# A two-layer recurrent trunk: the S5 branch loads a normed input that the GLA branch has written out

## The chip, the cores and the metric

The kernel runs on one core of one Trainium2 chip. The metric is the time of one execution on the device in microseconds (us). The kernel before takes 3261.68 us (median of three runs, 3260.92 to 3266.36).

The core has a matrix engine (TensorE, PE in the profile; PEld is its loading of weights), a vector engine (VectorE, DVE), a scalar engine (ScalarE, ACT), a general one (GpSimd, POOL), and SyncE (SP), which here issues nearly all DMAs. SBUF is the memory on the chip from which the engines work; DRAM is the large memory behind the DMAs.

## The reference, cut to what matters

One inference step of a trunk with two layers, on a prompt of 2048 tokens and 8 single sample tokens, with D_MODEL = 1024. The even layer norms its input, projects it, and runs two branches side by side on the same normed input: GLA (gated linear attention, 4 heads) and S5 (a diagonal state space model with 32 groups of 16 channels). Each branch ends in its half of one output projection, and both are added to the residual. The odd layer is a gated DeltaNet.

```
def rmsnorm(x, w):
    xf = x.astype(jnp.float32)
    y = xf * lax.rsqrt(jnp.mean(xf * xf, axis=-1, keepdims=True) + EPS)
    return (y * w.astype(jnp.float32)).astype(x.dtype)

h = rmsnorm(x, norm_w)              # both branches read this h
p = h @ w_in_even                   # q, k, v, r, gate code | S5 u, S5 gate
x = x + concat(gla(p) * silu(r), s5(p) * silu(gate)) @ w_out_even
```

The second half of this listing is written in short; the first is the reference's own text.

## The kernel before, in words

Tokens lie along the free axis as 2056 columns (8 samples, then 2048 of the prompt), features along the 128 partitions in 8 tiles of 128. Every product is made three times in parts to keep fp32 precision: a value is split into a high part (rounded to fp32r) and a low part (the rest), of the activations (`Hh`, `Hl`, or `Oh`, `Ol` for the output projection) and of the weights (`whl`), and PE adds hi*hi, hi*lo and lo*hi in one `pmm` tile (`dense_steps`, L93 in the profile). Weights are loaded as `raw` once, split by ACT (L319) and POOL (L320), stored to DRAM as `split` (L323), and loaded later from there as `whl` (L314, 512 KB each). `whl` has five buffers.

The even layer goes through the columns twice. GLA takes four blocks (520, 512, 512 and 512 columns): `gla_entry` transposes the input into `xT`, stores it in DRAM as `xs_d[0]` (L706), makes the norm's factor `rr`, stores one row of it in DRAM as `rr_d` (L716), makes the normed value `xn` (L721) and splits it into the block's tiles `Hh` and `Hl`. From there come GLA's products; `gla_out` ends the block: a product of `Oh`, `Ol` with the output weights, a load of the residual `res` (L1062, 256 KB), an addition on DVE (L1064), and a store to `xs_d[1]` (L1066). The addition reads the `pmm` tile, so it also frees it for PE.

S5 takes two halves. Half 0 has 1032 columns, worked in products of 392, 384 and 256 columns; half 1 has 1024, in two of 512. `s5_entry` makes the half's normed input again, in pieces of 264 or 256 columns: it loads `rr` (L1104) and, in two loads of 4 feature tiles, `xb` (L1107, 512 or 528 KB), and `normed` multiplies (POOL, L646), rounds to the high part (4 instructions on ACT, L648) and takes the low part (4 on DVE, L649). Then follow `s5_u` (the u products, the first with 392 columns), the scans, `s5_glu`, and the S5 half of the output projection (`ev` in `s5_glu`: load of `res` L1377, addition L1378, store to `xs_d[2]` L1379), whose tiles `oh`, `ol` are further buffers of the names Oh and Ol.

The order on PE is set by a weaver that runs these functions as generators side by side: a generator waits for an event that another posts, or says how many us its step is thought to take (the table `LAT`). The other engines are ordered by a scheduler from the same program. SP issues its DMAs in order on 8 lanes in turn; a DMA waits for the one eight before it, so at most eight are under way. The buffers `Hh`, `Hl` of S5 come free in half 0 when the last GLA chain closes its pool, and in half 1 when the glu products of half 0 (which keep `y5` and `yy` in the same two names) are done.

Of the kernel before, what the change touches and what calls it, by code (L numbers as in the profile page):

```python
# [35 lines left out]
C3 = float(np.float32(TWO_PI - C1 - C2))  # L36
MAGIC = 12582912.0

LAT = dict(gates=11, conv=5, kconv=8, snorm=5.25, z=2.04, tp=3, qtp=1, mt=18, grow=5, blocks=9, sub=3, dve=1.02, act=0.675,
           gchain=0.9, gload=1.2, gsample=15, columns=0.9, hout=3, gsplit=3.57, inv1=1.53, inv2=1.3, inv3=0.9,  # L40
           inv4=0.837, inv5=0.796, inv6=0.972, chain1=0.972, chain2=0.729, chain3=0.837, split=1.95, sload=2.66,
           cout=2.25, norm=5.5, load=2, us=3.74, sq=4, out=3.24, entry=9.6, x=1.88, gentry=7.98, make=30, far=8,
           pr=1.5, gate=9, lvl1=4.73, lvl=1.8, gnorm=6.8, scan=2.33, tab=10, entry5=8, glu=3, gelu=1.5, ysum=6)
LEAD = (750, 400)
HA, HL, GA = 6, 6, 2
SMB = 3
# [93 lines left out]
def tile_trunk(ctx, tc, A, O):  # L140
# [27 lines left out]
    def pieces(blk):  # L168

        ns, off, T, _ = bounds(blk)  # L170
        out, o = [], 0
        for c in range(0, blk[1], 2):
            k = min(2, blk[1] - c)
            w = P * k + (ns if c == 0 else 0)
            out.append((o, w, c, k))
            o += w
        return out
# [98 lines left out]


    xs_d = [dram.tile([P, KD, TT], F32, name="xs_d%d" % i) for i in range(3)]
    rr_d = dram.tile([1, TT], F32, name="rr_d")
    yp_d = dram.tile([S, D], F32, name="yp_d")  # L280
    ys_d = dram.tile([NSM, D], F32, name="ys_d")
    vs_d = [dram.tile([NSM, GDV], F32, name="vs_d%d" % h) for h in range(GH)]
# [390 lines left out]
    def gla_entry(gp, blk):  # L673

        ns, off, T, subs = bounds(blk)
        hi = gp.tile([P, KD, TG], F32R, tag="Hh", name="Hh")
        lo = gp.tile([P, KD, TG], F32R, tag="Hl", name="Hl")
        HG[blk] = hi, lo
        cl = cols(blk)
        if blk[0] == 0:  # L680
            with tc.high_priority(offset=tc.cur_priority):
                xload(blk, 0)
                row0 = gp.tile([P, P], F32, tag="rr", bufs=2, name="row0")[:KD]
                nc.sync.dma_start(row0, A["norm_w"][0].rearrange("(n p) -> n p", p=P))
                for j in range(1, len(cl)):
                    xload(blk, j)
                turn = vectors()
                pt = ptp()
                pe.transpose(pt[:, :KD], row0, ident[:KD, :KD])
                nc.vector.tensor_copy(nw0, pt[:, :KD])  # L690
        for j, (o, rows, ix) in enumerate(cl):
            x, xT = xload(blk, j), []
            if j:
                yield LAT["x"]
            for i4 in range(0, KD, 4):
                pt = ptp()
                p3 = pt[:, :4 * rows].rearrange("p (i t) -> p i t", i=4)
                for i in range(4):
                    pe.transpose(p3[:, i], x[:, (i4 + i) * P:(i4 + i + 1) * P], ident[:rows, :rows])
                tag = ("xT", "qe", "ket", "pt")[j % 4] if blk[0] == 0 else "xT"  # L700
                xT.append(gp.tile([P, 4, P], F32, tag=tag, bufs=2, name="xT")[:, :, :rows])
                if i4:
                    nc.vector.tensor_copy(xT[-1], p3)
                else:
                    nc.scalar.activation(xT[-1], p3, AF.Copy)
                nc.sync.dma_start(xs_d[0][:, i4:i4 + 4, off + o:off + o + rows], xT[-1])  # L706
            if j + 2 < len(cl):
                xload(blk, j + 2)
            yield LAT["pr"]
            if ix == 3:  # L710
                turn()
            pr = pmm()[:, :rows]
            pe.transpose(pr, rsx[:rows, ix:ix + 1].to_broadcast([rows, P]), ident[:rows, :rows])
            rr = gp.tile([P, P], F32, tag="rr", bufs=2, name="rr")[:, :rows]
            nc.scalar.activation(rr, pr, AF.Copy)
            nc.sync.dma_start(rr_d[0:1, off + o:off + o + rows], rr[0:1])  # L716
            for i4 in range(0, KD, 4):
                xn = gp.tile([P, 4, P], F32, tag="xn" if blk[0] else "kt", bufs=1 if blk[0] else 3,
                             name="xn")[:, :, :rows]
                for i in range(4):  # L720
                    nc.vector.scalar_tensor_tensor(xn[:, i], xT[i4 // 4][:, i], nw0[:, i4 + i:i4 + i + 1], rr,  # L721
                                                   op0=OP.mult, op1=OP.mult)
                split(hi[:, i4:i4 + 4, o:o + rows], lo[:, i4:i4 + 4, o:o + rows], xn,
                      nc.vector if blk[0] or i4 else nc.gpsimd)
            for (_, _, c, k) in subs:
                if blk[0] == 0 and c + k == ix:
                    weave.post(("gsub", c), LAT["gentry"])
                    weave.post(("gentry", 0))
        if blk[0] == 0:
            chunk_mask()  # L730
            pmask.update({s: block_mask(s, False, "pm%d" % s) for s in LEVELS})
        if blk[0]:
            weave.post(("gentry", GBLK.index(blk)), LAT["gentry"])
        yield LAT["gentry"]
        if blk[0]:
            yield "gz", GH * GBLK.index(blk) - 1
        yield from low_rank(gp, blk, hi, lo)
        weave.post(("lr", GBLK.index(blk)), LAT["dve"])
# [357 lines left out]
    def s5_entry(sp, half):  # L1096
        blk = SBLK[half]
        ns, off, T, subs = bounds(blk)
        hi = sp.tile([P, KD, TS], F32R, tag="Hh", name="Hh")
        lo = sp.tile([P, KD, TS], F32R, tag="Hl", name="Hl")  # L1100
        H5[half] = hi, lo
        for (o, w, c, k) in pieces(blk):
            rr = sp.tile([P, SWP], F32, tag="rr", bufs=1, name="rr")[:, :w]
            nc.sync.dma_start(rr, rr_d[0:1, off + o:off + o + w].to_broadcast([P, w]))  # L1104
            for i4 in range(0, KD, 4):
                xb = sp.tile([P, 4, SWP], F32, tag="xb", bufs=2, name="xb")[:, :, :w]
                nc.sync.dma_start(xb, xs_d[0][:, i4:i4 + 4, off + o:off + o + w])  # L1107
                normed(hi[:, i4:i4 + 4, o:o + w], lo[:, i4:i4 + 4, o:o + w], xb, rr, nw0[:, i4:i4 + 4], nc.vector)
            yield 0.0

    def s5_u(sp, half, ct, late):
# [214 lines left out]
    def s5_glu(sp, half):  # L1326
# [39 lines left out]
        yield from blocks_steps(A["s5_w_glu"][0], 4, 4, yh, yl, subs, ev_glu)  # L1366
        weave.post(("glu", half))
        if last:
            sp.close("sil", "entry", "main", "early")
            dp.open("main", "left")  # L1370
            weave.post("dnmain")
        sq = sp.tile([P, TS], F32, tag="sq", bufs=1, name="sq")
# [18 lines left out]
        if ns:  # L1391
# [7 lines left out]

    apart = dict(out=("xin", "thr", "res"), out2=("Oh", "Ol"), ext=("res2",))  # L1400
    gp = Phase(tc, "gla", h=("Hh", "Hl"), **apart)
    sp = Phase(tc, "s5", early=("Hh", "Hl", "h0"), entry=("xb", "rr"),
               start=("Q", "rt", "rows", "ldt", "ev", "dt", "drow", "prm", "x0", "x1", "h0s", "hr"),
               tabs=("q", "kp", "pp", "v0", "v1", "bx", "by", "cx", "cy", "xx", "xy", "y1", "y2", "dd", "smI", "smC", "smR"),
               up=("upad", "bsm"), sq=("sq",), sil=("sil", "hn", "hm", "hos"), **apart)
# [39 lines left out]
    def gla_entries():  # L1445
        for i, blk in enumerate(GBLK):
            if i:
                yield "gtail", i - 1
            yield from gla_entry(gp, blk)
            if i == 0:  # L1450
                yield "gsample", GH - 1
            if i + 1 < nb:
                xload(GBLK[i + 1], 0)
                xload(GBLK[i + 1], 1)
# [17 lines left out]
    def gla_chains():  # L1472
        for g, blk, h in gsteps:
            yield "gpre", g
            yield from gla_chain(gp, blk, h, g)
            weave.post(("gchain", g), LAT["gsplit"])
        for h_ in range(GH):
            nc.sync.dma_start(O[2][0, 0, h_], gS[h_])
        gp.close("main")
        sp.open("early", "left")  # L1480
        sp.open("entry", "left")
        weave.post("early5")

    def gla_outs():
# [24 lines left out]
    def s5_dense():  # L1509
        yield "early5"  # L1510
        yield "tabs"
        sp.open("sq", "right")
        sp.open("sil", "right")
        S5["h0"] = sp.tile([P, 2, SG, NSM], F32, tag="h0", bufs=1, name="h0")
        nc.sync.dma_start(S5["h0"], h0_d)
        delta_masks()
        for half in range(len(SBLK)):
            if half:
                yield "glu", half - 1
                yield "hn", half - 1  # L1520
                sp.close("up")
                sp.open("entry", "left")
            yield from s5_entry(sp, half)
            if half == 0:
                sp.close("entry")
                sp.open("main", "left")
                sp.open("up", "left")
            weave.post(("main5", half))
            yield LAT["entry5"]
            late = []  # L1530
            for ct in range(4):
                yield from s5_u(sp, half, ct, late)
            for ct in range(4):
                yield from after(s5_sg(sp, half, ct), late)
            weave.post(("H5", half))
# [805 lines left out]
```

## Time and profile before

| | before |
|---|---|
| median of three runs | 3261.68 us (3260.92 to 3266.36) |
| the profiled execution | 3250.56 us |
| its span, first to last instruction | 3248.8 us |
| PE busy | 2955.9 us, 91% of the span |
| DVE, ACT, POOL busy | 2224.4, 1255.7, 995.0 us |
| DMA | 602.96 MB, mean 186 GB/s |

The profile is one execution. Its busy times are sums per engine; the views by stretch and by wait say where PE stood and for whom. Times are from the span's start. The even layer takes about the first 1500 us: the GLA blocks start at about 0, 400, 650 and 900 us, S5's half 0 at 1174 us and half 1 at 1425 us.

### The profile page before, as it was taken

The page shows a single profiled execution, that of the slowest core. Times are in us where ns is not written, and L with a number is a line of the kernel's source. Part 1 is how long each engine was busy: PE and PEld are TensorE (multiplying, and loading weights), DVE is VectorE, ACT ScalarE, POOL GpSimd, SP SyncE. Part 2 cuts the span into 40 slices and gives each one's busy share as a digit, 9 for nine tenths or more (in the row PEclk, how much of TensorE's full clock was granted, in tenths as well). Part 3 has the DMA queues.
Part 4 walks back from the last instruction along what each step waited for, and adds up shares of the span by engine and source line. Part 5 has one row for each costly group of instructions (what it writes and reads, how often), then busy time and mean ns, then how long its engine had stood idle before and what let it go on. Part 6 is the DMA issues. An engine that isn't in the chain of part 4 may idle for free.

```text
span 3248.8 us, 53026 instructions
## 1 busy us (share of the span) xinstructions
PE 2955.9 (91%) x18425; PEld 2497.5 (77%) x18425; DVE 2224.4 (68%) x5715; ACT 1255.7 (39%) x3321; POOL 995.0 (31%) x1236
## 2 busy tenths in 40 slices
PE   6888799999999989978988888899998999999998
PEld 5877678777778768877767888877887788787886
DVE  7766556645444546765867888867887678857885
ACT  5443343323323323241134444443444344434442
POOL 6565444322202222240034444431112121211111
PEclk8898899999999999989999999999999999999999
DMA  7565965673483485664466566676444844475446
GB/s 216 190 209 177 297 184 148 190 256 126 136 276 126 133 287 153 200 202 148 155 198 216 172 193 185 190 230 221 139 147 140 270 146 145 125 234 192 141 139 191
DMA packets 398232, 602.96 MB, mean 186 GB/s; under 512 B 62521, under 2 KB 257964, under 8 KB 397828
## 3 DMA queue, kind: packets, MB, share of 16 engines
q1 hardware_dynamic: 394902, 589.98, 57.3%
q0 software_dynamic: 2560, 8.42, 0.9%
q8 instruction: 145, 2.38, 0.3%
q10 hardware_dynamic: 502, 1.17, 0.1%
q14 instruction: 123, 1.01, 0.1%
HBM read 433.31 MB, written 166.34 MB: 185 GB/s over the span
## 4 chain that ended last, share of the span: by engine, by line
PE 35%; DVE 15%; DMA 4%; issue 3%; ACT 2%; POOL 1%; SPq 0%; POOLq 0%; DVEq 0%; ACTq 0%
PE pmm L93 23%; PE prc L93 5%; PE ptp L97 2%; PE pch L93 2%; DVE yc L1692 2%; PE ppo L93 2%; DVE z L1237 1%; DVE z L1247 1%; DVE Hl L649 1%; DMA out<-yt 1%; DMA LB<-md_d 1%; DVE z L1243 1%; DMA whl<-split 1%; DVE z L1238 0%; DVE z L1248 0%
## 5 line engine op out<-in xcount | busy, mean ns | idle before, releaser
L93 PE MATMUL pmm<-Hh,whl 128*128 128x512 f32 (+4 forms) x5200 | 1597.3, 370 | 42.8 <-ACT pre L1682 13.2
L93 PEld LDWEIGHTS pmm<-Hh,whl 128*128 128x128 f32 x5200 | 951.2, 193 | 173.8 <-ACT pre L1682 14.8
L93 PE MATMUL pmm<-Hl,whl 128*128 128x512 f32 (+5 forms) x2640 | 937.0, 355 | 5.6 <-DVE Hl L649 4.2
L93 PEld LDWEIGHTS pmm<-Hl,whl 128*128 128x128 f32 (+1 forms) x2640 | 506.5, 192 | 55.6 <-DVE Hl L649 6.0
L93 PE MATMUL pmm<-Oh,whl 128*128 128x512 f32 (+2 forms) x1120 | 354.3, 379 | 30.5 <-DVE res L1064 13.4
L320 POOL TENSOR_TENSOR whl<-raw,whl 128x512 fp32r<-128x512 f32 (+1 forms) x176 | 232.3, 1322 | 203.9 <-ACT whl L319 194.9
L93 PEld LDWEIGHTS pmm<-Oh,whl 128*128 128x128 f32 x1120 | 211.3, 200 | 65.7 <-DVE res L1064 16.9
L1692 DVE SCALAR_TENSOR_TENSOR yc<-pre,cvec,yc 128x512 f32<-128x512 f32 (+1 forms) x288 | 228.8, 795 | 43.2 <-ACT yc L1690 40.5
L93 PE MATMUL pmm<-Ol,whl 128*128 128x512 f32 (+2 forms) x560 | 203.3, 363 | 0.6 <-DVE Ol L370 0.6
L319 ACT ACTIVATE whl<-raw 128x512 fp32r<-128x512 f32 (+1 forms) x176 | 108.5, 618 | 127.4 <-PE pmm L93 78.0
L93 PEld LDWEIGHTS pmm<-Ol,whl 128*128 128x128 f32 x560 | 112.6, 201 | 11.4 <-DVE Ol L370 1.7
L907 DVE TENSOR_TENSOR dlt<-b 128x512 f32<-128x512 f32 x112 | 87.5, 782 | 39.8 <-ACT E L914 38.9
L93 PE MATMUL pmm<-oh,whl 128*128 128x512 f32 (+3 forms) x320 | 93.6, 370 | 18.3 <-DVE res L1378 15.4
L908 ACT ACTIVATE E<-dlt 128x256 f32<-128x256 f32 x112 | 47.4, 423 | 156.1 <-DVE dlt L907 32.3
L1682 ACT ACTIVATE pre<-pmm 128x512 f32<-128x512 f32 (+1 forms) x120 | 61.1, 510 | 115.4 <-PE pmm L93 115.1
L646 POOL TENSOR_TENSOR xb<-xb,rr 128x1024 f32<-128x1024 f32 (+1 forms) x32 | 76.9, 2412 | 90.9 <-DMA xb<-xs_d 40.4
L1968 ACT ACTIVATE jk<-ppo,rq 128x128 bf16<-128x128 f32 x128 | 46.7, 365 | 140.2 <-PE ppo L93 139.1
L1685 POOL COPY halo<-pre 128x3 f32<-128x3 f32 x96 | 22.3, 232 | 241.0 <-ACT pre L1682 240.3
L1064 DVE TENSOR_TENSOR res<-pmm,res 128x512 f32<-128x512 f32 (+2 forms) x80 | 46.2, 584 | 68.6 <-PE pmm L93 50.0
L1729 ACT ACTIVATE jk<-ptp 128x128 bf16<-128x128 f32 x256 | 70.8, 277 | 53.8 <-PE ptp L97 48.3
L275 POOL TENSOR_TENSOR s<-s,mhalf 128x4 f32<-128x4 f32 (+2 forms) x41 | 40.6, 989 | 162.6 <-DVE s L274 160.7
L1695 ACT ACTIVATE th<-yc 128x512 f32<-128x512 f32 (+1 forms) x96 | 61.0, 635 | 73.1 <-DVE yc L1692 72.8
(1527 smaller groups left out, 6103.8 us busy)
## 6 DMA issues: line engine op xcount, KB each, us to landing
whl<-split SPq DMA_DIRECT2D x460, 512.0 KB
split<-whl SPq DMA_DIRECT2D x168, 512.0 KB
res<-xs_d SPq DMA_DIRECT2D x88, 256.0 KB
sm<-s5m SPq DMA_DIRECT2D x32, 514.0 KB
raw<-in_w_in_even SPq DMA_DIRECT2D x64, 256.0 KB
xs_d<-res SPq DMA_DIRECT2D x64, 256.0 KB
raw<-in_w_in_odd SPq DMA_DIRECT2D x64, 256.0 KB
LB<-md_d SPq DMA_DIRECT2D x64, 256.0 KB
```

Source lines behind the costliest of these rows:

```text
L93: return self.e.matmul(out, w, x, **kw)
L97: return self.e.transpose(out, x, ident)
L319: nc.scalar.activation(t[:, 0, :m], raw, AF.Copy)
L320: nc.gpsimd.tensor_tensor(t[:, 1, :m], raw, t[:, 0, :m].bitcast(F32), op=OP.subtract)
L646: nc.gpsimd.tensor_tensor(xb, xb, rr.unsqueeze(1).to_broadcast(list(xb.shape)), op=OP.mult)
L907: nc.vector.tensor_tensor(d3, b3, b3[:, :, s - 1:s].to_broadcast([P, nb_, 2 * s]), op=OP.subtract)
L908: nc.scalar.activation(E3[:, :, s:], d3[:, :, s:], AF.Exp, scale=IS)
L1682: nc.scalar.activation(pre[:, X0 + c * P:X0 + (c + k) * P], ps[:, n0:], AF.Copy)
L1692: nc.vector.scalar_tensor_tensor(yv, pre[:, i:W - 3 + i], convw[:, ti, i:i + 1], yv, op0=OP.mult, op1=OP.add)
L1695: nc.scalar.activation(t[:, 3:W], yv, AF.Tanh, scale=0.5)
L1729: nc.scalar.activation(jk, pt[:, c * P:(c + 1) * P], AF.Square, accum_out=ss[:, c:c + 1])
L1968: nc.scalar.activation(jk[:rows], po[:rows, c * P:(c + 1) * P], AF.Square, scale=rq[:rows, c:c + 1], accum_out=s1[:, c:c + 1])
```

## The change

`gla_entries` stores the block's tiles `Hh` and `Hl` to two new DRAM tensors `xn_d[0]` and `xn_d[1]`, in four steps of two stores each, a step thought to take `LAT["keep"]` = 15 us. That is 8 stores of 512 KB (520 KB in block 0) a block, 32 in all, 16.8 MB. `s5_entry` loads from there, per product's columns and per 4 feature tiles, the high and the low part: 12 loads in half 0 (four of 784 KB, four of 768 KB, four of 512 KB) and 8 of 1 MB in half 1, again 16.8 MB. Gone are, in S5, the 8 loads of `rr`, the 16 loads of `xb` (8.4 MB), 16 multiplications on POOL, 64 instructions on ACT and 64 on DVE, and in GLA the 17 stores of `rr_d`. The pool `entry` (buffers `xb`, `rr`) is gone, and with it the closing of that pool before `main` and `up` open. `normed` stays for the DeltaNet layer.

```
+            off, T = bounds(blk)[1:3]                        # gla_entries, after gla_entry(gp, blk)
+            for k in range(0, KD, 2):
+                yield LAT["keep"]
+                for t, to in zip(HG[blk], xn_d):
+                    nc.sync.dma_start(to[:, k:k + 2, off:off + T], t[:, k:k + 2, :T].bitcast(F32))
...
-            nc.sync.dma_start(rr_d[0:1, off + o:off + o + rows], rr[0:1])      # gla_entry
...
-        for (o, w, c, k) in pieces(blk):                                       # s5_entry
-            rr = sp.tile([P, SWP], F32, tag="rr", bufs=1, name="rr")[:, :w]
-            nc.sync.dma_start(rr, rr_d[0:1, off + o:off + o + w].to_broadcast([P, w]))
+        for (o, w, c, k) in subs:
             for i4 in range(0, KD, 4):
-                xb = sp.tile([P, 4, SWP], F32, tag="xb", bufs=2, name="xb")[:, :, :w]
-                nc.sync.dma_start(xb, xs_d[0][:, i4:i4 + 4, off + o:off + o + w])
-                normed(hi[:, i4:i4 + 4, o:o + w], lo[:, i4:i4 + 4, o:o + w], xb, rr, nw0[:, i4:i4 + 4], nc.vector)
+                for t, src in ((hi, xn_d[0]), (lo, xn_d[1])):
+                    nc.sync.dma_start(t[:, i4:i4 + 4, o:o + w].bitcast(F32), src[:, i4:i4 + 4, off + o:off + o + w])
             yield 0.0
...
-LAT = dict(... mt=18, grow=5, ... entry5=8, ...)
+LAT = dict(... mt=18, keep=15, grow=5, ... entry5=14, ...)
```

The order of PE's matmuls is the same before and after, instruction by instruction. SP's is not; three places follow. Line numbers of the changed kernel are lower by 1 (L1061, L1065) or by 4 (L1373, L1375).

SP, where S5's half 0 enters, before: `h` is the S5 state of the samples, `xb` and `rr` the inputs of the norm, `res` and `xs_d_86` the residual of the last GLA block.

```order
L1515 DMA h_11954<-h_d 128x512
L1104 DMA rr<-rr_d 128x264
L1107 DMA xb<-xs_d_85 128x4x264 x2
L1066 DMA xs_d_86<-res 128x512
L1062 DMA res<-xs_d_86 128x512
L314 DMA whl<-split_4804 128x1024
L314 DMA whl<-split_4921 128x1024
L1066 DMA xs_d_86<-res 128x512
L1062 DMA res<-xs_d_86 128x512
```

SP, the end of the same stretch in the changed kernel: 8 loads of the parts of the 384 and 256 columns, three of `sm<-s5m` and three of `sm<-s5k` (S5's tables), three of `whl`, four stores of `xs_d`, one `res` and `h` have gone ahead, 25 DMAs from the first `Hh` to the `split` shown, both included; `xn_d_88` is the high part, `xn_d_89` the low.

```order
L318 DMA raw<-in_w_in_even 128x4x128
L323 DMA split_12171<-whl 128x1024
L1104 DMA Hh<-xn_d_88 128x4x392
L1104 DMA Hl<-xn_d_89 128x4x392
L1104 DMA Hh<-xn_d_88 128x4x392
L1104 DMA Hl<-xn_d_89 128x4x392
L318 DMA raw<-in_w_in_even 128x4x128
L323 DMA split_12178<-whl 128x1024
L1065 DMA xs_d_86<-res 128x512
L1061 DMA res<-xs_d_86 128x512 x3
```

The first piece and the last residual loads of GLA stood near each other at the head; now the 392 columns, which PE's first u product reads, are the last of the twelve parts, and the last three residual loads stand behind them. The tables `sm` and the parts of the later columns stand ahead of both.

SP in GLA's block 2, before: `whl` are the output weights, `s5m` and `q` stores and loads of S5's tables.

```order
L318 DMA raw<-in_w_in_even 128x4x128
L1066 DMA xs_d_86<-res 128x512
L599 DMA s5m<-smR 128x258
L1066 DMA xs_d_86<-res 128x512
L314 DMA whl<-split_4686 128x1024
L1062 DMA res<-xs_d_86 128x512
L314 DMA whl<-split_4693 128x1024
L1062 DMA res<-xs_d_86 128x512
L528 DMA q<-s5q 128x68
```

The same place in the changed kernel.

```order
L318 DMA raw<-in_w_in_even 128x4x128
L599 DMA s5m<-smR 128x258
L1450 DMA xn_d_88<-Hh 128x2x512 x2
L1450 DMA xn_d_89<-Hl 128x2x512 x2
L314 DMA whl<-split_4689 128x1024
L1061 DMA res<-xs_d_86 128x512
L1065 DMA xs_d_86<-res 128x512
L314 DMA whl<-split_4696 128x1024
L528 DMA q<-s5q 128x68
L1450 DMA xn_d_88<-Hh 128x2x512 x2
L1065 DMA xs_d_86<-res 128x512
L614 DMA s5m<-smC 128x128
```

The block's eight stores stand between the loads of weights and residuals that the block's output products take, four, then four again. In block 1 they stand around two `whl` loads in the same way, in block 3 in one row with single DMAs between, and in block 0 all eight follow one another.

SP, where S5's half 1 enters, in the changed kernel: `xs_d_87<-res` are stores, `res<-xs_d_86` loads of half 0's S5 output products.

```order
L1104 DMA Hh<-xn_d_88 128x4x512
L1375 DMA xs_d_87<-res 128x384
L1104 DMA Hh<-xn_d_88 128x4x512 x2
L1104 DMA Hl<-xn_d_89 128x4x512
L1104 DMA Hh<-xn_d_88 128x4x512
L1375 DMA xs_d_87<-res 128x256
L1104 DMA Hl<-xn_d_89 128x4x512
L1375 DMA xs_d_87<-res 128x392
L1373 DMA res<-xs_d_86 128x256
```

The same place before.

```order
L1379 DMA xs_d_87<-res 128x384
L1107 DMA xb<-xs_d_85 128x4x256
L1377 DMA res<-xs_d_86 128x256
L1107 DMA xb<-xs_d_85 128x4x256
L1379 DMA xs_d_87<-res 128x256
L1377 DMA res<-xs_d_86 128x392
```

Six loads of 1 MB stand together ahead of the next residual load, where residual loads and loads of 512 KB took turns. Two more loads of `Hl` stand further up, the first of them ahead of the last load of `sil` (the gate of half 0's last glu product), and it waits until that product has read `yy`.

## Rows read from the trace of the kernel before

**Rows 1.** The page: busy times, then the first DMA queue.
```profile
PE 2955.9 (91%) x18425; PEld 2497.5 (77%) x18425; DVE 2224.4 (68%) x5715; ACT 1255.7 (39%) x3321; POOL 995.0 (31%) x1236
...
q1 hardware_dynamic: 394902, 589.98, 57.3%
```

**Rows 2.** Waits of PE, 1140 to 1260 us: us in total, times, longest.
```profile
PE pmm L93 <- ACT Hh L648: 9.3, 3, 6.3
PE pmm L93 <- DVE res L1064: 5.0, 3, 3.0
PE pmm L93 <- DVE Hl L649: 3.7, 3, 2.3
```

**Rows 3.** Timeline of PE: start, us, instructions, in brackets the idle time before.
```profile
1200.44 0.42 PE L93 MATMUL pmm<-Hh,whl 128*128 128x392 f32 x1 [1.27 <-DVE res L1064]
...
1213.14 0.69 PE L93 MATMUL pmm<-Hh,whl 128*128 128x384 f32 x1 [6.25 <-ACT Hh L648]
...
1214.14 0.84 PE L93 MATMUL pmm<-Hh,whl 128*128 128x384 f32 x2
...
1215.11 0.84 PE L93 MATMUL pmm<-Hh,whl 128*128 128x384 f32 x2
...
1218.44 0.51 PE L93 MATMUL pmm<-Hh,whl 128*128 128x384 f32 x2
...
1218.97 0.51 PE L93 MATMUL pmm<-Hh,whl 128*128 128x384 f32 x2
...
1231.16 0.34 PE L93 MATMUL pmm<-Hl,whl 128*128 128x392 f32 x1
```

**Rows 4.** Stretches of 10 us: PE, PEld, DVE, ACT, POOL, clock, DMA share, GB/s.
```profile
1200.00:1210.00 10.00, 5.06 (x24) 4.11 (x24) 5.79 (x8) 3.36 (x7) 5.16 (x3) 1.00 1.07 376
...
1220.00:1230.00 10.00, 4.77 (x22) 4.25 (x22) 5.43 (x8) 4.71 (x12) 5.22 (x3) 0.70 0.33 93
```

**Rows 5.** The norm's instructions by line: ns of one (min/median/max), first and last start.
```profile
L646 POOL TENSOR_TENSOR xb<-xb,rr x32: 2339/2392/2659, 1182.4 to 2835.9; 128x1024 f32<-128x1024 f32 x28, 128x1056 f32<-128x1056 f32 x4
...
L648 ACT ACTIVATE Hh<-xb,nw x64: 492/494/514, 1184.9 to 1469.2; 128x256 fp32r<-128x256 f32 x56, 128x264 fp32r<-128x264 f32 x8
...
L649 DVE SCALAR_TENSOR_TENSOR Hl<-xb,nw,Hh x64: 468/474/2665, 1185.5 to 1470.3; 128x256 fp32r<-128x256 f32 x56, 128x264 fp32r<-128x264 f32 x8
```

**Rows 6.** Timeline of SP at the start of half 0.
```profile
1174.18 2.67 SPq L1107 DMA_DIRECT2D xb<-xs_d  x2
```

**Rows 7.** Waits of DVE, 1165 to 1240 us.
```profile
DVE hn L1311 <- DMA h<-h_d: 6.0, 1, 6.0
```

**Rows 8.** Waits of PE, 1400 to 1520 us.
```profile
PE pmm L93 <- DVE res L1378: 11.0, 5, 5.2
PE ptp L97 <- DVE hos L1321: 6.1, 1, 6.1
PE pmm L93 <- ACT thr L1359: 3.8, 2, 2.1
```

**Rows 9.** The output products of half 0's S5 part, columns as in rows 4.
```profile
1430.00:1480.00 50.00, 39.00 (x221) 37.51 (x220) 34.28 (x61) 19.88 (x46) 18.99 (x10) 0.90 0.83 264
```

**Rows 10.** Stretches of GLA blocks 0, 1, 2, 3, columns as in rows 4.
```profile
40.00:60.00 20.00, 17.02 (x140) 16.09 (x138) 11.66 (x61) 15.02 (x26) 12.18 (x10) 1.00 0.54 170
400.00:440.00 40.00, 33.88 (x153) 26.14 (x154) 19.93 (x54) 15.39 (x33) 16.23 (x32) 0.87 0.78 242
630.00:700.00 70.00, 61.38 (x256) 45.24 (x257) 36.24 (x101) 18.95 (x47) 15.77 (x38) 0.93 0.89 287
900.00:970.00 70.00, 66.07 (x292) 50.62 (x291) 33.41 (x71) 19.79 (x39) 6.48 (x7) 1.00 0.87 287
```

**Rows 11.** Waits of PE, 0 to 1170 us.
```profile
PE pmm L93 <- DVE res L1064: 13.3, 7, 3.7
...
PE pmm L93 <- DMA whl<-split: 1.9, 2, 1.1
```

More of the change, by code (lines that the diff above doesn't have):

```diff
@@ L37 @@
 MAGIC = 12582912.0
-LAT = dict(gates=11, conv=5, kconv=8, snorm=5.25, z=2.04, tp=3, qtp=1, mt=18, grow=5, blocks=9, sub=3, dve=1.02, act=0.675,
+LAT = dict(gates=11, conv=5, kconv=8, snorm=5.25, z=2.04, tp=3, qtp=1, mt=18, keep=15, grow=5, blocks=9, sub=3, dve=1.02, act=0.675,
            gchain=0.9, gload=1.2, gsample=15, columns=0.9, hout=3, gsplit=3.57, inv1=1.53, inv2=1.3, inv3=0.9,
@@ L42 @@
            cout=2.25, norm=5.5, load=2, us=3.74, sq=4, out=3.24, entry=9.6, x=1.88, gentry=7.98, make=30, far=8,
-           pr=1.5, gate=9, lvl1=4.73, lvl=1.8, gnorm=6.8, scan=2.33, tab=10, entry5=8, glu=3, gelu=1.5, ysum=6)
+           pr=1.5, gate=9, lvl1=4.73, lvl=1.8, gnorm=6.8, scan=2.33, tab=10, entry5=14, glu=3, gelu=1.5, ysum=6)
 LEAD = (750, 400)
@@ L278, in tile_trunk @@
     xs_d = [dram.tile([P, KD, TT], F32, name="xs_d%d" % i) for i in range(3)]
-    rr_d = dram.tile([1, TT], F32, name="rr_d")
+    xn_d = [dram.tile([P, KD, TT], F32, name="xn_d%d" % i) for i in range(2)]
     yp_d = dram.tile([S, D], F32, name="yp_d")
@@ L1368, in s5_glu @@
         if last:
-            sp.close("sil", "entry", "main", "early")
+            sp.close("sil", "main", "early")
             dp.open("main", "left")
@@ L1401, in tile_trunk @@
     gp = Phase(tc, "gla", h=("Hh", "Hl"), **apart)
-    sp = Phase(tc, "s5", early=("Hh", "Hl", "h0"), entry=("xb", "rr"),
+    sp = Phase(tc, "s5", early=("Hh", "Hl", "h0"),
                start=("Q", "rt", "rows", "ldt", "ev", "dt", "drow", "prm", "x0", "x1", "h0s", "hr"),
@@ L1480, in gla_chains @@
         sp.open("early", "left")
-        sp.open("entry", "left")
         weave.post("early5")
@@ L1521, in s5_dense @@
                 sp.close("up")
-                sp.open("entry", "left")
             yield from s5_entry(sp, half)
             if half == 0:
-                sp.close("entry")
                 sp.open("main", "left")
```

## The prediction

> **What bounds the kernel now.** I read the page first: PE is busy for 91% of the span, DVE for 68%, the large DMA queue takes 57% of the DMA engines' time [rows 1]. So what the change takes from POOL, ACT and DVE counts only where PE stood waiting for it, and what it adds to the DMAs counts only where PE comes to wait for a transfer. Then I read PE's waits where the norm works. In half 0 PE waits 9.3 us for the high part (L648) and 3.7 us for the low part (L649), and 5.0 us for the additions of GLA's last residuals [rows 2]. PE's timeline shows what is lost: the first u product begins at 1200.44 us, its 384-column part comes 6.25 us late at 1213.14, and the second product begins just before 1231.16 [rows 3]. The stretches say that the DMAs are not idle meanwhile: in 1200 to 1210 their share is 1.07 at 376 GB/s; only in 1220 to 1230 is it down to 0.33 [rows 4]. I take 376 GB/s as the full rate. Last I read PE's waits around half 1 and the stretches in which the GLA blocks will make their stores; the reader is to look there for waits that the loads of residuals explain, and for room at the DMAs.
>
> **What goes.** 16 multiplications of 2.39 us on POOL (38 us), 64 instructions of 0.494 us on ACT (32 us) and 64 of 0.474 us on DVE (30 us) [rows 5]. None is itself on PE's path; the worth is PE's waits. The 17 small stores of `rr_d` are one SP issue each; I cost them at nothing.
>
> **Half 0.** How long would the first u product take if nothing held it? Three matmuls of 384 columns take 0.53 us at the full clock, from 1218.44 to 1218.97, so 0.46 ns a column, and 0.97 us at the half clock, 1214.14 to 1215.11, so 0.84 ns [rows 3]. The product is 24 matmuls over 1032 columns: 24 x 1032 x 0.46 ns = 11.4 us. It takes some 30.6 us now, so 19 us are lost, 13 in waits for the norm [rows 2] and the rest to the half clock after them.
>
> The change does not simply give these back. The loads start when the buffers come free, as the first `xb` does at 1174.18 [rows 6]. The order shows what stands ahead of the 392-column parts, which the first product needs first: 8.45 MB of parts in all, 2.0 MB of `sm` tables, 1.6 MB of `whl`, 1.0 MB of stores and 1.3 MB of other DMAs, 14.4 MB up to the last 392-column load; the first of the three last residual loads stands at 15.7 MB, two DMAs of weights and a store after them. At 376 GB/s these are 38 and 42 us, so the 392-column parts land at about 1212 and the residual at about 1216, some 1 to 2 later with what is under way when they start. The three additions that wait for those residuals each hold a `pmm` buffer, and the last GLA output product cannot start before one is free. So PE stops after the last but one output product (before, all were done at 1199) and resumes at about 1217.5. The last product's 12 matmuls of 512 columns take 12 x 512 x 0.84 ns = 5.2 us at the half clock, on which PE stands after such an idle time (1214.14 against 1218.44 [rows 3]), and then come 11.4 us of u, of which some us at the half clock add 1 to 2. The u product ends at 1235 to 1236 instead of 1231: **+4 us**. Bounds: at 10% more bytes per us everything comes 4 us earlier (0); with 3 us more of backlog and the state load of 6.0 us [rows 7] later for DVE too, +10. Below: if the residual loads are not what holds the last product, it runs beside the loads and u starts at 1212 to 1214, which ends it at 1224 to 1226, -6.
>
> The Trainium skill ("DMA: Bandwidth & Descriptors", Where 436 GB/s comes from) gives about 358 GB/s per core as what binds transfers between DRAM and SBUF, below the 435 of the fabric. The trace of this core shows 376 for 10 us [rows 4], so here the trace decides; by 358 the sum for half 0 would be 2 us worse.
>
> **Half 1.** The loads cannot start before half 0's glu products are read, as the order has it, at about 1418. The first `Hl` load now stands ahead of the last `sil` load and waits for that product; PE waited 3.8 us for `thr` here already [rows 8]; the sil load comes after 1 MB, 2.8 us at the full rate: I take +2. Then six loads of 1 MB stand ahead of the next residual load of the output products: 6.3 MB, 17 us; some four products' residuals are already in. With a product's share of the 50 us shown at some 2.8 us each I estimate that PE stands 7 us once. Against this the 11.0 us in which PE waited for the additions L1378 [rows 8], with L649 on the same engine between them, largely go, and POOL and ACT are free of 8 and 32 instructions. 2 + 7 - 11 = **-2 us**. Bounds: -11 (both costs hidden, all additions prompt) to +9 (both costs, nothing gained, because the additions were late for their loads: the share of the DMAs was 0.83 [rows 9]). The 6.1 us for `hos` [rows 8] are a chain between PE and DVE; I leave them.
>
> **GLA.** This is the part that the change's purpose does not speak of, and where I expect the loss. Each block gets 8 stores of 4.19 MB together (4.26 in block 0), 11.2 us of the full rate. They are read by nothing for long, but SP issues them in order between loads that PE's products wait for. I work out what room is there: 20 us at a share of 0.54 leave 9.2 us free in block 0, 40 us at 0.78 leave 8.8 in block 1, 70 us at 0.89 leave 7.7 in block 2, 70 us at 0.87 leave 9.1 in block 3 [rows 10]. In block 0 the stretch behind is as free and the weights run ahead: nothing. In the others 2.4, 3.5 and 2.1 us don't fit, and since five `whl` buffers are about as much prefetch as one burst of four stores delays (5 x 12 matmuls x 0.23 us = 14 us against 5.6), I charge just what doesn't fit: **+8 us**. Here whatever waits is a wait for `whl` (1.9 us so far) or for additions whose `res` comes late (13.3 us so far) [rows 11]. Bounds: 0, if the prefetch hides it all; +22, if blocks 2 and 3, whose output products take their weights and residuals at a share near 0.9, lose the whole 11.2 us each. Small gains from the missing `rr_d` stores I put at nothing.
>
> **Sum.** +4 - 2 + 8 = +10 us. The profiled execution took 3250.56 us and would take 3261; it is 11 us quicker than the median of the runs, to which I add the same 10: 3271.7, and I say **3271 us**.
>
> **The rivals.**
> 1. *The waits go and the stores are hidden (faster).* For it: PE waits 13 us for the norm in half 0 and 11 us for additions behind L649 in half 1 [rows 2, 8], and in the GLA blocks PE waited for `whl` only 1.9 us in 1170 us [rows 11], so prefetch has been deep enough. Against it: share 1.07 at 376 GB/s while the norm works [rows 4], and the residual loads behind the 392-column parts. Half 0 -4, half 1 -8, GLA +1: -11, 3251 us.
> 2. *No change.* The stores cost half of what I charge, half 0 comes out at 0, half 1 at -4: 0, 3262 us.
> 3. *The DMAs become the bound in GLA (much slower).* Blocks 2 and 3 lose the full 22 us, block 1 half of its 11.2, half 0 +4, half 1 -2: +30, 3292 us. It decides once the output products' loads stand at the full rate without the stores already; the shares of 0.87 to 0.89 are means over 70 us, with room in some places and none in others.
> 4. *The change does not remove the wait in half 0*, because it never was the norm's: the loads of `xb` are 4.2 MB, the parts are 8.45 MB, and they pass the same queue. This is inside my forecast and not a time of its own.
>
> The same skill page (Issuing engines are not separate DMA queues) says that all DMAs end on the same 16 engines, whoever issues them. That is a rule against moving work from three engines with room to the one resource that half 0 fills; no run here shows yet what it costs.
>
> **How the numbers follow.** My forecast 0.42, rival 1 0.30, rival 2 0.18, rival 3 0.10. A measurement of this kernel can tell about 0.2%, 6.5 us, from no change. The forecast's own range is 3262 to 3281, with one part in seven of it within 0.2%; a tenth of rival 1 lies there too. Faster 0.29, same 0.24, slower 0.47. The range that should hold 8 in 10 reaches from most of rival 1 to most of rival 3: 3247 to 3289 us.
>
> **What would show it.** In the profile after: the first u product should start near 1222 plus what the GLA blocks lost before it, with a wait of PE for the additions of GLA's residuals of 10 to 18 us in place of those for L648 and L649; if it starts before 1214 by that reckoning, the order of the loads does not matter. The waits of PE up to the start of half 0 should have grown by some 8 us, for `whl` or for `res` additions in blocks 2 and 3; if PE's work there ends at the same time as before, GLA costs nothing and rival 1 is near. In half 1 PE should have one wait of about 7 us for an addition whose `res` is late, and few others. I am wrong altogether if the GLA blocks change by more than 22 us, or if half 0 ends its u product more than 6 us earlier.

## The result, and the profile after

The changed kernel takes 3296.94 us (median of 6 runs, 3287.37 to 3306.56) where the kernel before takes 3259.86 in the same comparison: a ratio of 1.0124, 95% interval 1.0103 to 1.0146. It is slower, as forecast, but by some 37 us instead of 10, and above the range of 3247 to 3289 us. Its profiled execution took 3298.70 us, with a span of 3297.0.

PE runs its matmuls in the same order in both kernels, so the k-th matmul of one trace can be laid beside the k-th of the other, and the difference of their starts says how much later the changed kernel is at that place. This table is worked out that way from the traces: what each stretch of the first profile of before (its times head the columns) takes longer, in us. The second row is a second profile of before, and shows what is chance.

| | GLA, 0-1170 | half 0, 1170-1250 | 1250-1400 | half 1, 1400-1520 | 1520-1680 | DeltaNet, 1680-3240 | all |
|---|---|---|---|---|---|---|---|
| before, second profile (e5) | 3.7 | 0.2 | 1.8 | -2.2 | -0.8 | 12.5 | 15.2 |
| changed kernel | 19.6 | 8.3 | -1.1 | 13.9 | 0.2 | 7.4 | 48.4 |
| changed, second profile (e6) | 19.9 | 7.9 | -0.9 | 13.8 | -0.8 | 5.5 | 45.4 |

So the change costs about 8 us in half 0, 14 in half 1, and in GLA 16 to 20 of which a part is chance: e11 and e12 below have GLA's code as before and stand at 2.5 and -4.1 there. The DeltaNet layer, whose code is the same, takes 12 us longer in the second profile of before too: the first was a quick execution, and nothing there is the change's.

The page of the changed kernel, its busy times and first DMA queue: the three engines have less to do, as planned, by 34, 27 and 47 us [rows 1], and PE's work is the same within 6.

```profile
PE 2961.5 (90%) x18425; PEld 2501.3 (76%) x18425; DVE 2190.7 (66%) x5651; ACT 1228.8 (37%) x3257; POOL 948.2 (29%) x1220
...
q1 hardware_dynamic: 404532, 614.18, 58.3%
```

PE's waits in half 0 of the changed kernel, 1160 to 1260 us. Those for the norm [rows 2] are gone; in their place stand one of 17.8 us for an addition and 8.1 us for weights.

```profile
PE pmm L93 <- DVE res L1063: 20.7, 2, 17.8
PE pmm L93 <- DMA whl<-split: 8.1, 2, 5.7
```

DVE's waits, 1190 to 1250 us: the addition was late because its residual was, and the state load came 13.6 us late where it had been 6.0 [rows 7].

```profile
DVE res L1063 <- DMA res<-xs_d: 23.3, 2, 22.8
DVE hn L1307 <- DMA h<-h_d: 13.6, 1, 13.6
```

The stretches of half 0 and half 1 of the changed kernel, columns as in [rows 4]. Both show PE all but standing still while the DMAs run at a share above 1 and 349 to 398 GB/s; before, PE was still busy 4.77 us in its worst stretch [rows 4].

```profile
1200.00:1210.00 10.00, 4.26 (x17) 3.14 (x16) 0.69 (x1) 0.63 (x1) 1.28 (x1) 0.85 1.08 368
1210.00:1220.00 10.00, 7.11 (x23) 5.14 (x21) 1.88 (x4) 0.63 (x1) 1.27 (x1) 0.81 1.08 349
1220.00:1230.00 10.00, 1.86 (x7) 1.05 (x6) 0.00 (x0) 0.63 (x1) 0.92 (x1) 0.70 1.06 387
1230.00:1240.00 10.00, 0.00 (x0) 0.00 (x0) 0.00 (x0) 0.00 (x0) 0.34 (x1) 0.50 1.06 383
...
1460.00:1470.00 10.00, 1.41 (x8) 1.08 (x7) 0.00 (x0) 0.07 (x1) 2.67 (x3) 0.82 1.05 398
1470.00:1480.00 10.00, 2.47 (x8) 2.47 (x9) 0.84 (x2) 0.39 (x1) 0.00 (x0) 0.50 1.06 391
```

DVE's timeline in half 1: after the addition at 1457.90 the next has to wait until 1477.06 for its residual.

```profile
1457.90 0.56 DVE L1374 TENSOR_TENSOR res<-pmm,res 128x384 f32<-128x384 f32 x1 [0.39 <-PE pmm L93]
1459.02 0.55 DVE L1379 TENSOR_TENSOR sq<-sq,prc 128x384 f32<-128x384 f32 x1 [0.56 <-ACT prc L1377]
1477.06 0.42 DVE L1374 TENSOR_TENSOR res<-pmm,res 128x256 f32<-128x256 f32 x1 [17.48 <-DMA res<-xs_d]
```

PE's waits, 1420 to 1545 us: the additions' 11.0 us [rows 8] became 20.7; the waits for `hos` and `thr` grew by 1.3 and 0.3.

```profile
PE pmm L93 <- DVE res L1374: 20.7, 5, 16.1
PE ptp L97 <- DVE hos L1317: 7.4, 1, 7.4
PE pmm L93 <- ACT thr L1355: 4.1, 2, 3.3
```

The GLA blocks of the changed kernel, the stretches of [rows 10]: the shares of 0.54, 0.78, 0.89 and 0.87 are now 0.92, 0.96, 0.89 and 0.91, and PE is busy for 1.7 to 5.2 us less in each. The windows are those of the clock. Moved by the 9, 13.5 and 18.5 us by which PE is late there, the last three show shares of 0.96, 0.96 and 0.98, and PE is busy for 2.5, 4.7 and 1.2 us less.

```profile
40.00:60.00 20.00, 15.32 (x109) 14.51 (x108) 10.71 (x50) 14.96 (x23) 10.61 (x9) 0.83 0.92 333
400.00:440.00 40.00, 28.67 (x137) 22.47 (x136) 19.62 (x51) 15.28 (x32) 10.13 (x20) 0.86 0.96 320
630.00:700.00 70.00, 57.25 (x240) 42.02 (x241) 39.64 (x114) 18.65 (x52) 15.07 (x35) 0.90 0.89 293
900.00:970.00 70.00, 61.73 (x276) 47.00 (x276) 33.96 (x79) 14.71 (x36) 3.09 (x5) 0.98 0.91 309
```

### The profile page after: what moved, and what is told of

Same layout as the page of the kernel before. It is cut to its first block, busy times and chain, and to the rows that moved or that the text cites. A ratio compares the mean times of both kernels' runs of the same rounds, so it can differ in the third digit from the quotient of the medians.

```text
span 3297.0 us, 52863 instructions
## 1 busy us (share of the span) xinstructions
PE 2961.5 (90%) x18425; PEld 2501.3 (76%) x18425; DVE 2190.7 (66%) x5651; ACT 1228.8 (37%) x3257; POOL 948.2 (29%) x1220
## 4 chain that ended last, share of the span: by engine, by line
PE 35%; DVE 15%; DMA 5%; issue 3%; ACT 2%; POOL 1%; SPq 1%; POOLq 0%; DVEq 0%; ACTq 0%
PE pmm L93 24%; PE prc L93 5%; PE ptp L97 2%; PE pch L93 2%; PE ppo L93 2%; DVE yc L1690 2%; DMA out<-yt 1%; DVE z L1233 1%; DVE z L1243 1%; DMA LB<-md_d 1%; DMA xs_d<-res 1%; DVE z L1239 1%; DVE Hl L649 1%; DVE z L1234 0%; DVE z L1244 0%
## 5 line engine op out<-in xcount | busy, mean ns | idle before, releaser
L93 PEld LDWEIGHTS pmm<-oh,whl 128*128 128x128 f32 x320 | 60.6, 198 | 37.0 <-DVE res L1374 26.8
(1525 smaller groups left out, 6006.1 us busy)
```

What stands on the lines that cost most here:

```text
L93: return self.e.matmul(out, w, x, **kw)
```

## The experiments

Each ran beside the kernel before, whose median is given with it. The figures by stretch are differences to the first profile of before, as in the table.

**e1, the stores alone.** To the kernel before:

```
+                for t, to in zip(HG[blk], xn_d):
+                    nc.sync.dma_start(to[:, k:k + 2, off:off + T], t[:, k:k + 2, :T].bitcast(F32))
```

> The kernel before with the 32 stores of the normed parts added in the GLA blocks (16.8 MB that nothing reads); S5 makes its own norm as before. Theory (three losses: stores in GLA, loads in half 0, loads in half 1): PE reaches the end of GLA (1170 us of before) 15 to 20 us late, as in the changed kernel, half 0 and half 1 then cost nothing more: +15 to +20 us, 3275 to 3280. Rival (the stores are hidden, and the 19 us by which the changed kernel was late there are the spread between executions): 0 to +5 us.

Measured: 3271.98 us against 3254.87, ratio 1.0044 (1.0029 to 1.0058), +17 us. GLA +13.6, half 0 0.0, half 1 +1.2. What the stores cost they cost in GLA, and nothing in the halves. The rival falls.

**e2, the loads alone.** To the changed kernel, whose stores are taken out; both parts are read from the un-normed input, so the values of the norm are left out:

```
-                for t, src in ((hi, xn_d[0]), (lo, xn_d[1])):
+                for t, src in ((hi, xs_d[0]), (lo, xs_d[0])):
```

> The changed kernel without the stores; S5's 20 loads keep their size and place but read the un-normed input for both parts (the values are wrong, the bytes are the same). Theory: GLA as before, half 0 +8 and half 1 +13 us by the place of PE's matmuls: +18 to +24 us, 3278 to 3284. Rival (the loads read what was stored late, so the loss in the halves came from the stores): 0 to +5 us, 3260 to 3265, or a gain of some 10 us by the waits for the norm that are gone.

Measured: 3284.45 against 3254.87, 1.0082 (1.0058 to 1.0107), +30. Half 0 +8.3, half 1 +10.5, as the loads' theory has it. DeltaNet's +10.6 lies near the second profile of before (12.5). GLA's +7.8 is above what profiles of its unchanged code show (-4.1 to 3.7). There are no stores here, but the 17 stores of `rr_d` are gone as in the changed kernel, and SP, DVE, ACT and POOL run GLA in another order from about 20 us on. The total was 6 above what was expected.

**e3, the loads on POOL's queue.** In the changed kernel, for the 20 loads:

```
-                    nc.sync.dma_start(t[:, i4:i4 + 4, o:o + w].bitcast(F32), src[:, i4:i4 + 4, off + o:off + o + w])
+                    nc.gpsimd.dma_start(t[:, i4:i4 + 4, o:o + w].bitcast(F32), src[:, i4:i4 + 4, off + o:off + o + w])
```

> The changed kernel with S5's 20 loads issued from POOL's queue, so that no residual or weight load of SP stands behind them; bytes as in the changed kernel. Theory of order (the residual loads wait their turn behind the loads): PE's waits of 17.8 us in half 0 and 16.1 us in half 1 for residual additions shrink to under 5 us each; half 0 and half 1 come out between -8 and +5 us each against before, the total near +15 to +22 us, 3275 to 3282. Rival theory of bytes (what counts is that 8.4 MB more a half pass the same DMA engines): the waits move to the normed parts and the sum stays, 3292 to 3300.

Measured: 3298.15 against 3254.87, 1.0126 (1.0100 to 1.0152). Half 0 +8.2, half 1 +11.3: nothing is won in half 0 and little in half 1. The waits of PE in half 0, 1180 to 1270 us, only change their name:

```profile
PE pmm L93 <- DMA whl<-split: 24.3, 1, 24.3
PE pmm L93 <- DVE res L1063: 5.2, 1, 5.2
```

SP's timeline shows how: none of S5's loads stands ahead of the weights on this queue any more, but the issue of each of these two weight loads now takes SP 6 to 7 us. What holds SP there is not shown.

```profile
1198.78 6.18 SPq L314 DMA_DIRECT2D whl<-split  x1
...
1207.04 7.36 SPq L314 DMA_DIRECT2D whl<-split  x1
```

The theory of order, which was mine, falls for the sum; the order only chooses which wait shows.

**e4, the stores on POOL's queue.** In the changed kernel, for the 32 stores:

```
-                    nc.sync.dma_start(to[:, k:k + 2, off:off + T], t[:, k:k + 2, :T].bitcast(F32))
+                    nc.gpsimd.dma_start(to[:, k:k + 2, off:off + T], t[:, k:k + 2, :T].bitcast(F32))
```

> The changed kernel with the 32 stores issued from POOL's queue instead of SP's. Theory of order: the GLA blocks lose 0 to 6 us instead of 19, the halves lose their 21 as before: +21 to +27, 3281 to 3287. Theory of bytes: GLA still loses 15 to 20, 3292 to 3300. In both POOL's own work may be delayed by the issuing, which would show as waits for kt or whl.

Measured: 3284.87 against 3254.87, 1.0092 (1.0062 to 1.0122), +30. GLA still loses 16.6, so there too the queue is not what counts. Half 0 +9.4, half 1 +6.5: with the same loads half 1 costs between 6.5 and 13.9 us in these runs, and what makes the difference is not shown.

**e5 and e6, both kernels again,** for a second profile each.

> The kernel before once more, for a second profile: how far the places of PE's matmuls in GLA, the halves and the DeltaNet layer differ between two executions of one kernel. Theory (the first profile was a quick execution: 3250.56 against medians of 3255 to 3262): it reaches the end of GLA 4 to 8 us later than the first, the DeltaNet layer takes 4 to 8 us more, the two halves the same within 2 us. Rival (the profile is typical and the differences in GLA and DeltaNet belong to the changed kernel): all within 2 us.

> The changed kernel once more, for a second profile. Theory: half 0 again some 8 us and half 1 some 11 to 13 us longer than in the kernel before, GLA 13 to 20 us longer than in the first profile of before, DeltaNet anywhere within 8 us. Rival (the halves' loss is chance too): it differs by more than 4 us.

Measured: 3265.76 and 3295.69; the stretches are in the table. The losses in the halves repeat within 0.4 us, GLA's within 0.3. What GLA differs between two profiles of before is 3.7 us, and DeltaNet 12.5, more than was expected.

**e7, the high part alone.** In the changed kernel the loads of the low part become zeros, which leaves the low part's share out of the result:

```
+                nc.sync.dma_start(hi[:, i4:i4 + 4, o:o + w].bitcast(F32), xn_d[0][:, i4:i4 + 4, off + o:off + o + w])
+                nc.gpsimd.memset(lo[:, i4:i4 + 4, o:o + w].bitcast(F32), 0.0)
```

> The changed kernel in which S5 loads only the high part; the low part is set to zero by POOL (the low part's products are left out of the result, all matmuls stay), so 4.2 MB a half less pass the DMAs. Theory of bytes: PE's long waits shrink by 4.2 MB at 0.37 MB a us, 11 us each, less what then waits for something else: half 0 from +8 to between -5 and 0 against before, half 1 from +12 to between -5 and +3; with GLA's 13 to 17 us as in the changed kernel, total 3265 to 3276. Rival (the place of the loads ahead of the last residual loads matters, not the bytes): the waits stay over 12 us, total above 3285.

Measured: 3263.07 against 3251.59, 1.0049 (1.0033 to 1.0065), +11. Half 0 -4.3 and half 1 -7.5, where the changed kernel has +8.3 and +13.9: 12.6 and 21.4 us for 4.2 MB less each. At 376 GB/s [rows 4] 4.2 MB take 11.2 us, so half 1 wins more than the bytes alone; the rest is not taken apart. In half 1 the waits of PE for late additions, 1400 to 1530 us, are all but gone:

```profile
PE ptp L97 <- DVE hos L1317: 7.2, 1, 7.2
PE pmm L93 <- ACT oh L1358: 6.1, 1, 6.1
...
PE pmm L93 <- DVE res L1374: 1.9, 2, 1.0
```

With e3 this settles the halves: with half the bytes the change would be a gain there, and the loads that are left stand where they stood on the queue. GLA, with all stores, lost 23.2.

**e8 and e10, one store of the unsplit value.** To the kernel before; S5 loads as many bytes of `xb` as before, no `rr`, and only splits what it loads; e10 stores over POOL's queue.

```
+                nc.sync.dma_start(xn_d[:, i4:i4 + 4, off + o:off + o + rows], xn)
...
-                normed(hi[:, i4:i4 + 4, o:o + w], lo[:, i4:i4 + 4, o:o + w], xb, rr, nw0[:, i4:i4 + 4], nc.vector)
+                split(hi[:, i4:i4 + 4, o:o + w], lo[:, i4:i4 + 4, o:o + w], xb, nc.vector)
```

> A version that could beat both: GLA stores the normed value once, in fp32, before its split (34 stores, 8.4 MB, as each tile is made), S5 loads it as it loaded the input before (16 loads of the same size and place) and only splits it (one wide instruction on ACT and one on DVE a load; no multiplication on POOL, no factor). Theory of bytes: half 0 and half 1 between -10 and 0 against before, since the DMAs there carry the same and the chain behind a load is shorter; GLA loses about half of what the 16.8 MB cost, 6 to 9 us; total -4 to +9, 3251 to 3264. Rival (stores in GLA cost by their number and place, not their bytes): GLA loses 13 us or more, total 3265 or more.

> The version that stores the unsplit normed value once, with those 34 stores on POOL's queue. Theory (in the version on SP the norm's instructions waited for the store to release their tile, and the store waited its turn on SP): GLA loses 8 to 15 us instead of 36, the halves keep their -10 and -4, total -6 to +5 against before. Rival (the engines are shared, so the tile is held as long): GLA loses over 25, total +10 or more.

Measured: e8 3272.92 against 3251.59, 1.0062 (1.0041 to 1.0083); e10 3275.27 against 3252.28, 1.0076 (1.0052 to 1.0099). The halves gain 9.8 and 4.6, and 10.5 and 5.3: the norm's chain was worth that much when the bytes stay as they were. But GLA loses 36.5 and 44.6, in part at least because the store holds the tile `xn` that the next norm instruction needs. DVE's waits of e8 from 410 to 600 us have it, and in the same stretch PE waited 10.2 us at once for the high part that follows:

```profile
DVE xn L720 <- DMA xn_d<-xn: 8.4, 4, 4.0
```

The theory of e10, that POOL's queue frees the tile sooner, falls.

**e9 and e13, half of the stores.** As e1, with the high part's stores alone (e9) or the low part's (e13):

```
-                for t, to in zip(HG[blk], xn_d):
+                for t, to in zip(HG[blk][:1], xn_d):           # e9
+                for t, to in zip(HG[blk][1:], xn_d[1:]):       # e13
```

> The kernel before with the 16 stores of the high part alone (8.4 MB that nothing reads), at the places where the changed kernel has them; S5 makes its norm as before. Theory of bytes (each stored MB costs the GLA blocks about 1 us): GLA and the whole +6 to +9 us, half of what the 32 stores cost, 3258 to 3261 where before has 3252. Rival (the stores cost by holding up what stands behind them on SP, a burst being a burst): +12 us or more. It also says what of the 36 us that GLA lost with one store of the unsplit value, 8.4 MB too, came from the tile that such a store holds.

> The kernel before with the 16 stores of the low part alone (8.4 MB that nothing reads), where the changed kernel has them; S5 makes its norm as before. The 16 stores of the high part cost 0 to 5 us, all 32 cost 17. Theory of room (the free DMA time in the blocks takes up about 8 MB, only what goes beyond is paid): the low stores alone cost as little as the high ones, GLA -2 to +6 us, total 0 to +7, 3252 to 3259. Rival of waiting (the low part is made last, on DVE or POOL, and its store holds SP while it waits for it): GLA +9 to +14 us, total +9 or more.

Measured: 3257.34 against 3252.28, 1.0015 (0.9998 to 1.0031), and 3258.94 against 3252.71, 1.0015 (0.9997 to 1.0033); GLA -1.8 and +6.2. So neither part is the costly one, and a wait for the low part is not the cause. Some 5 and 6 us against 17 together looks like more than the sum, as if the first stores found room; but the intervals leave the plain sum possible, and that stays open.

**e11 and e12, more buffers for the norm's input.** To the kernel before (e12: `xb` with `bufs=4`, `rr` as it was):

```
-            rr = sp.tile([P, SWP], F32, tag="rr", bufs=1, name="rr")[:, :w]
+            rr = sp.tile([P, SWP], F32, tag="rr", bufs=2, name="rr")[:, :w]
-                xb = sp.tile([P, 4, SWP], F32, tag="xb", bufs=2, name="xb")[:, :, :w]
+                xb = sp.tile([P, 4, SWP], F32, tag="xb", bufs=3, name="xb")[:, :, :w]
```

> The kernel before with a third buffer for the norm's input and a second for its factor, no stores and no bytes added: S5's loads are asked for earlier, the chain POOL, ACT, DVE stays. Theory (in half 0 of before the loads of xb waited 11.8 us for a buffer, and PE 13 us for the norm): half 0 gains 3 to 8 us, half 1 0 to 3, GLA and DeltaNet unchanged within the spread: -3 to -10 us. Rival (the DMAs are full in that stretch, so earlier requests only delay the residuals, as in the changed kernel): half 0 within 2 us or slower.

> The kernel before with four buffers for the norm's input and one for its factor. Theory as for three buffers: half 0 gains 3 to 8 us unless the single buffer of the factor holds the pieces back; in half 1 all first four loads come before the glu products end, 0 to 4 us. Rival: within 2 us, or slower because four loads stand ahead of the residuals.

Measured: 3251.76 against 3252.28, 1.0000 (0.9987 to 1.0012), and 3260.25, 1.0026 (1.0013 to 1.0038). With three buffers half 0 changes by -1.1 us. PE's waits, 1160 to 1260 us, say why:

```profile
PE pmm L93 <- DVE res L1064: 8.2, 3, 3.9
PE pmm L93 <- DVE Hl L649: 4.4, 4, 1.7
PE pmm L93 <- ACT Hh L648: 2.7, 2, 1.5
```

The wait for the high part fell from 9.3 to 2.7 us, that for additions rose from 5.0 to 8.2 [rows 2]. The rival of this pair holds in its number. Its reason, that the DMAs are full, is not shown to be the only one: DVE's part of the norm was slow there as well, 4.82 us for four L649 from 1207.71 on, where one takes 0.474 in the median [rows 5]. With four buffers half 0 changes by -0.3 and half 1 loses 5.2.

**e14, the low part in bf16.** The changed kernel with

```
+    xn_d = [dram.tile([P, KD, TT], (F32, BF16)[i], name="xn_d%d" % i) for i in range(2)]
```

and the low part's DMAs on POOL's queue.

> A version that could be better than the changed kernel: the low part lies in DRAM in bf16, its stores and loads go over POOL's queue and change the type on the way, so the low part's DRAM bytes are halved (4.2 MB stored, 2.1 MB a half loaded); the low part's own low bits are lost. Theory (what counts is the bytes at DRAM): half 0 between -2 and +4 against before, half 1 between 0 and +8, GLA +5 to +10, total +5 to +18. Rival (what counts is the bytes at SBUF, or DMAs that change the type move more slowly): the halves lose 20 us or more as in the changed kernel, total +30 or more. Neither theory has it faster than before.

Measured: 3282.87 against 3252.71, 1.0078 (1.0051 to 1.0106), +30; half 0 +4.9, half 1 +7.1, GLA +21.0, where 5 to 10 was expected. The halves lie between what the bytes at DRAM and those at SBUF would give, so this doesn't tell them apart; in GLA a quarter of the stored bytes less saved nothing.

No version here beats the kernel before.

## Why the prediction was wrong

**What held.** The direction, and the ground for it: PE comes to stand behind bytes. Half 0 went as worked out: the wait moved from the norm to the last residuals (17.8 us, expected 10 to 18), the last output product took 5.3 us at the half clock (1242.03 to 1247.32 in the trace, 5.2 worked out), and then came the u product. The term was +4 and measured +8.3, inside its bounds. The lines of PE's timeline:

```profile
1242.03 0.79 PE L93 MATMUL pmm<-Oh,whl 128*128 128x512 f32 x1 [17.77 <-DVE res L1063]
...
1247.32 0.53 PE L93 MATMUL pmm<-Hh,whl 128*128 128x392 f32 x1
```

What was too small is the time until the residual lands: 15.7 MB were counted up to it, and it landed at 1241 where 1236 follows from my count and the 19 us by which GLA was late. From the first load of the parts, at 1192.60, to 1241 the DMAs moved 17.9 MB (369 GB/s over 48.4 us). The 2.2 MB more were under way before or issued behind; how much of each is not shown.

**The step that failed: half 1, -2 forecast, +14 measured.** Two terms of it were mis-sized. I had 7 us for the wait behind the six loads, because some four products' residuals were to be in already. Five additions did run from 1449.12 to 1457.90, but SP issued the six loads only from 1454.91 on, so after the one at 1457.90 nothing is left to add until the loads have passed: 16.1 us of wait, about the whole of 6.3 MB at 391 to 398 GB/s. SP's timeline has the first and the last of the six, and the residual load behind them:

```profile
1454.91 0.37 SPq L1104 DMA_DIRECT2D Hh<-xn_d  x1
...
1464.43 0.55 SPq L1104 DMA_DIRECT2D Hl<-xn_d  x1
...
1467.63 0.56 SPq L1373 DMA_DIRECT2D res<-xs_d  x1
```

And I let the 11.0 us of other waits for additions go almost entirely; 4.6 stayed (20.7 less 16.1). 16 instead of 7 and 5 instead of nothing are 14 of the 16 us by which the term was off. The wait for `thr` behind the `sil` load, costed at +2, grew by 0.3, and that for `hos`, which I left alone, by 1.3. What is left, some 2 us, may be PE's clock, 0.63 from 1515 to 1525 us where the kernel before has 0.92 for about the same products (1475 to 1485); no run takes it apart.

**GLA: +8 forecast, 14 to 20 measured.** The sum of e1 is 17 by the medians and 13.6 in its profile, and the changed kernel stands at 16 to 20 in GLA against the two profiles of before. Block by block (from 0, 400, 650 and 900 us of before) it loses 9.4, 4.1, 5.0 and 1.1 us, in its second profile 8.2, 5.0, 4.9 and 1.9, where I had 0, 2.4, 3.5 and 2.1. So the term that failed most is block 0, which I put at nothing because the stretch behind its stores is as free. There the eight stores follow one another, the share from 40 to 60 us is 0.92 where I read 0.54, and PE waits for a load of S5's state (`hr`) and for `vtmp`, for which it had waited 2.2 us before. PE's waits, 40 to 130 us:

```profile
PE ptp L97 <- ACT vtmp L797: 8.3, 2, 7.1
PE ptp L97 <- DMA hr<-in_state_s_im: 3.5, 1, 3.5
```

At 60 us PE is 15.8 us late, and at 120 all but 3.1 of it is made good, so a late stretch here is not yet a loss. In e4 PE is only 2.8 us late at 60, and GLA loses 16.6 all the same.

Not all of GLA's loss need be the stores'. At 35 us, before the first of them is issued (37.30), the changed kernel is 1.5 us late and e2, which has none, 1.9; e1, e5, e11 and e12 lie between -0.7 and 0.5. In block 0 as a whole e2 loses 4.5 us and e1 2.6. The changed kernel and e2 share the missing `rr_d` stores, which I put at nothing, and the other order of SP, DVE, ACT and POOL that goes with them. No run has these alone, so their share stays open.

What I named as the form of the loss is there in block 2. PE's waits for additions, 630 to 740 us, before and in the changed kernel:

```profile
PE pmm L93 <- DVE res L1064: 4.1, 2, 3.7
PE pmm L93 <- DVE res L1063: 9.1, 5, 4.3
```

I take the mistake to be one of method: the free share of 40 to 70 us was read as room for stores that come in bursts of four and eight. No run spread the same stores out, so this is argued and not shown.

**The rivals.** Rival 4, which I put aside as no time of its own, is half right. For it, e11 took away most of PE's wait for the norm's high part and won nothing, since PE then waited longer for additions. Against it, the wait was in part the norm's: e8, with the same bytes and a shorter chain behind them, gains 9.8 and 4.6 in the halves, and e7, with the same bytes and no norm, 4.3 and 7.5 (both come out of GLA late, by 36.5 and 23.2 us). It is the other 4.2 MB a half that turn this gain into a loss. Rival 1 took PE's 13 and 11 us of waits for the norm's price. Rival 3 had nearly the size, +30, but in the wrong place: it has 28 us in GLA and 2 in the halves, the runs have 14 to 20 and 22.

**Order or bytes.** I argued half 0 and half 1 from the place of the loads on SP's queue. e3 shows that the place isn't the cause: on another queue the same bytes cost 8.2 and 11.3. The Trainium skill ("DMA: Bandwidth & Descriptors", Issuing engines are not separate DMA queues) says that DMAs end on the same 16 engines whoever issues them. The traces agree, with a share of 1.03 to 1.08 in these stretches on either queue. I had cited it against the move of work to the DMAs, and not drawn from it that the place on a queue would matter little. e7 is the direct measure: 4.2 MB less in each half turn +8.3 and +13.9 into -4.3 and -7.5.

## What to carry to other kernels

A wait for an engine's result is worth paying for in bytes only if the DMAs beside it have room: read the DMA share of the same 10 us before swapping arithmetic for bytes, and price the bytes at the full rate against everything that PE needs in that stretch. A shorter chain with the same bytes did gain here (e8). Once the DMAs were full, moving the loads to another queue changed the name of the wait in half 0 and not its length. Room for stores I would now read burst by burst, and not from a mean over a stage; how far that helps no run here shows.

## What was not expected of the hardware

Loads on POOL's queue take their share at once from SP's DMAs: in e3 a `whl` of 512 KB made PE wait 24.3 us. DMAs that change the type (e14) show a DMA share of 1.67 at 385 GB/s in one stretch of 10 us, so their share can't be read as that of the others. And one kernel's time spreads more than 0.3%: the kernel before gave 3243.83 to 3268.43 us in 15 runs, with most of the difference between two profiles (12.5 of 15.2 us) in the DeltaNet layer.
